# Which products of the MLP stay in PSUM: first and second products of both column groups, in place of four plain sums, with other orders of the pieces

## The chip, the cores and the metric

One core of a Trainium2 chip runs the kernel. The metric is the device time of one execution in microseconds (us); the median of 3 runs before is 1192.7 us.

## The reference

One decoder layer in fp32 over 256 tokens and 16 meta tokens, width D = 2048. After the mixers, which the change does not touch, comes the MLP with 8192 hidden columns:

```python
u = rms_norm(h, g_pre_mlp[l])
f = jnp.square(jax.nn.relu(u @ w_up[l])) @ w_down[l]
h = h + rms_norm(f, g_post_mlp[l])
return h[:, N_META:]
```

## The kernel before

**Numbers.** A weight chunk is 1 MB (128x2048 fp32). SP loads it into one of 5 raw rooms (L1510). ACT rounds it to its high part (`hi`, L1554), DVE subtracts that from the raw chunk (`lo`, L1558). These two halves go into one of four slots: three pairs, and a fourth called `fourth_pair`, which never serves the up projection. TensorE multiplies activations, split in the same way, with both halves.

**The MLP.** Its hidden columns are cut into 8 pieces of 1024. The up projection of a piece has eight chunks U0a0 to U1b1, each 32 matmuls into the banks u0 and u1, which ACT (L1638) and DVE (L1645) read after every second chunk. The down projection has an inner size of 1024 per piece, in two halves, 2 token blocks and 4 column blocks of 512. Of all but the first and the last piece it is done by a seven-product scheme for 2x2 blocks: P1 to P7 for the column blocks 0 and 1, Q1 to Q7 for 2 and 3. Each such product is 12 matmuls 128x512 by `down` (L1771). The weights of P6, P4, Q6 and Q4 are sums that DVE forms in place (L1571, as raw_a<-raw_a,raw_c). Those of P5, P7, Q5 and Q7 are sums that DMAs with an accumulate form, issued on POOL (L1576): the chunk B12, for one, is loaded, then B22 is accumulated onto it, and that is P7's weight. The activations' forms are made by DVE and ACT (L1720 to L1741). X and Y are plain products: 24 matmuls with one raw chunk for both token blocks.

**Banks and sums.** TensorE writes 8 PSUM banks: u0 and u1, four sums x00, x01, x10, x11 for the column blocks 2 and 3 (named acc_up in the trace), and two shared banks a and b. P products go to a and b. After each P product one DVE operation, a *give* (L1804), reads the bank and adds it into `F` in SBUF. Several products add onto what already stands in the bank: P6, P7 and P4 onto a, so that P7 may start only when the give of P6 has read a. Of the Q products Q2, Q3 and Q4 go straight to the x banks. After Q1, Q5, Q6 and Q7 ACT copies bank a or b to SBUF (`st_Q`, L1813), and DVE adds this copy to one or two x banks (L1818). After the last products come squares, a row factor r, and the final multiply-adds with their stores.

**Order.** The strings PLAIN, BLOCKS and LAST_PIECE give the order of products. The class Plan (L23) keeps PE's and SP's order as written and orders the work of DVE, ACT and POOL by costs and by the due times of what waits. An engine works through its list in that order.

Of the kernel before, what the change touches and what calls it, by code (L numbers as in the profile page):

```python
# [15 lines left out]
P = 128  # L16
CK = 4
CW = 512
# [97 lines left out]
def hybrid_block(ctx: ExitStack, tc: tile.TileContext, ins: dict, out: bass.AP):  # L116
# [213 lines left out]
    def load_rows(queue, *names):  # L330
        rows = tmp.tile([48, P], F32, tag="g", name=f"rows_{names[0]}")
# [27 lines left out]
    pre_rows = load_rows(nc.scalar, "g_pre_mix")  # L359
# [13 lines left out]
    other_rows = load_rows(nc.gpsimd, "pool_scale", "b_dw", "conv_ln_g", "conv_ln_b", "g_pre_mlp")  # L373
# [193 lines left out]
    def evac_g(j0):  # L567
        def f(j, acc):
            q = j0 + j
            g = tmp.tile([P, L], F32, tag="g", name=f"g_{q}")  # L570
# [854 lines left out]
    F_raw = big.tile([P, 2 * NT * D // 2], F32, tag="k8", bufs=2, name="F_raw")  # L1425
    F = F_raw[:, :NT * D // 2].rearrange("p (t n c) -> p t n c", t=NT, n=2)

    Q = F_raw[:, NT * D // 2:].rearrange("p (f k t) -> p f k t", f=4, k=KH)
    S3Q, S1Q, S4Q, SQ = range(4)
    S2Q = S3Q  # L1430
    room_of = {}
# [15 lines left out]
    PLAIN = "X3 X1 U0a0+ U0a1+ P1 U0b0+ U0b1+ X2 U1a0+ P5 U1a1+ U1b0+ P3 add:P P6 X4 P7 P2 P4"  # L1447
    BLOCKS = "U0a0+ P1 U0a1+ P5 U0b0+ P6 P3 add:P P7 U0b1+ P4 U1a0+ Q1 P2 Q3 U1a1+ U1b0+ Q5 Q2 add:Q Q6 Q4 Q7"
# [209 lines left out]
    def relu_squared(h, pr, i, s_name, box):  # L1658
# [21 lines left out]
        def q_(f):  # L1680
            return Q[:, f, ks, :]
# [22 lines left out]
    def into_forms(h, pr, i, s_name, box):  # L1704
        G, A, ks = forms[h], f"A{h}{pr}", slice(2 * pr, 2 * pr + 2)

        n = 2 if h or i == NP - 1 or "X1" in MODES[i] else 1

        def dst(part):
            return G[:, A1:A1 + n, ks, part, :]  # L1710

        def src():
            return box["s"].rearrange("p j (f t) -> p f j t", f=2)[:, :n]
        if i < NP - 1 and h == 1:
            def a_(f):
# [19 lines left out]

    def split_form(b, f, name, q, q_name):
        G = forms[b]
        src = [f"{q_name}{pr}" for pr in range(2)]
        plan.add("ACT", 0.53, lambda: nc.scalar.copy(G[:, f, :, 0, :], Q[:, q]),
                 reads=src, writes=(name,))  # L1740
        plan.add("DVE", 0.62, lambda: nc.vector.tensor_sub(  # L1741
            G[:, f, :, 1, :], Q[:, q], f32(G[:, f, :, 0, :])),
            reads=src + [name], writes=(name + "l",))

    def up_done(h, pr, i, accs, acc_names):
        if i == 0:
            n = 2 * h + pr
            up_pair(h, pr, i, accs, acc_names, f"F{n}", lambda: F[:, n // 2, n % 2, :])
# [6 lines left out]
    s_rooms = [Q[:, SQ].rearrange("p k t -> p (k t)")]  # L1755
# [31 lines left out]
    GIVES = {"P1": (0, 0, 1), "P2": (0, 0, 1), "P3": (0, 1, 1), "P4": (1, 0, 1),  # L1787
             "P5": (1, 1, 1), "P6": (0, 1, -1), "P7": (1, 1, -1)}
    GIVES_X = {"Q1": [("x00", 1)], "Q6": [("x10", -1)], "Q7": [("x01", 1), ("x11", -1)],
               "Q5": [("x10", 1), ("x11", 1)]}  # L1790
    given = set()


    def give(s, i):
        t, n, sign = GIVES[s]
        first_ = (t, n) not in given
        given.add((t, n))
        bank, dst, name = banks[BANK[s]], F[:, t, n, :], f"F{2 * t + n}"

        def f():  # L1800
            if first_:
                nc.vector.tensor_scalar_mul(dst, bank, float(sign))
            else:
                (nc.vector.tensor_add if sign > 0 else nc.vector.tensor_sub)(dst, dst, bank)  # L1804
        plan.add("DVE", 0.62, f, reads=(BANK[s], name), writes=(name,))

    def give_x(s):
        box = {}
        bank = BANK[s]

        def save():
            box["st"] = tmp.tile([P, CW], F32, tag="junk", bufs=1, name=f"st_{s}")
            nc.scalar.copy(box["st"], banks[bank])  # L1813
        plan.add("ACT", 0.5, save, reads=(bank,), writes=("junk",))
        for name, sign in GIVES_X[s]:
            def f(dst=banks[name], add_=(nc.vector.tensor_add if sign > 0 else
                                         nc.vector.tensor_sub)):
                add_(dst, dst, box["st"])  # L1818
            plan.add("DVE", 0.62, f, reads=("junk",), writes=(name,))
# [16 lines left out]

    def product_plain(m_, s, i):
        h, n = AT[s]
        for t, f in ((0, A1), (1, A2)):
            name = f"x{n - 2}{t}"  # L1840
            plan.add("PE", 2.72, lambda t=t, f=f, name=name: down(
                banks[name], split_at[m_], h, f, i == 0 and h == 0,
                h == 1 and i == NP - 1 - (n == 3)),
                reads=half_names(m_) + act_names(h, f), writes=(name,))


    LAST_BANK = {(0, 0): "a", (0, 1): "b", (1, 0): "u0", (1, 1): "u1"}

    def product_last(m_, s, i):
        h, n = AT[s]  # L1850
        for t, f in ((0, A1), (1, A2)):
            name = LAST_BANK[n, t]
            plan.add("PE", 2.72, lambda t=t, f=f, name=name: down(
                banks[name], split_at[m_], h, f, h == 0, h == 1),
                reads=half_names(m_) + act_names(h, f), writes=(name,))
        for t in range(NT if h == 1 else 0):
            name, blk = LAST_BANK[n, t], f"F{2 * t + n}"
            plan.add("DVE", 0.62, lambda t=t, name=name: nc.vector.tensor_add(
                F[:, t, n, :], F[:, t, n, :], banks[name]), reads=(name, blk), writes=(blk,))

    def product_block(m_, s, i):
        h, f = FORM[s]
        plan.add("PE", 2.72, lambda: down(banks[BANK[s]], split_at[m_], h, f, s in OPENS, True),
                 reads=half_names(m_) + act_names(h, f), writes=(BANK[s],))
        if s[0] == "P":
            give(s, i)
        elif s in GIVES_X:
            give_x(s)


# [12 lines left out]
    for j in range(4):  # L1883
        plan.add("PE", 1.36, last_of_first(j), reads=(f"hi{q0}", f"lo{q0}"),
                 writes=(f"x{j // 2}{j % 2}",))
# [9 lines left out]
    for pr in range(2):  # L1895
        up_done(0, pr, 0, accs[2 * pr:2 * pr + 2], [f"x{pr}{j}" for j in range(2)])
# [3 lines left out]
    for at_step[0], (s, i) in enumerate(steps):  # L1900
# [18 lines left out]
        {"U": product_up, "X": product_plain, "P": product_block, "Y": product_last,  # L1919
         "Q": product_block}[s[0]](m_, s, i)  # L1920
        m_ += 1
        if (s, i) == ("U1b1", 0):
# [30 lines left out]
    def times_g(t, n):  # L1953
# [3 lines left out]
            reads=(name, f"raw{room_g}"), writes=(f"out{t}{n}", name if n < 2 else f"raw{room_f}"))  # L1957
# [103 lines left out]
```

## Time and profile before

| what | value |
|---|---|
| runs, us | 1189.87, 1192.7, 1196.38 |
| profiled execution | 1189.83 us, of which 1188.1 us span |
| mean granted clock of TensorE | 0.998 |
| PE, DVE, ACT, POOL busy | 1174.9, 1033.6, 688.8, 44.9 us |
| DMA | 272.91 MB, mean 230 GB/s |

The span runs from the first to the last instruction. Busy is the time an engine spends in instructions; of PE the ends are modelled. "a <- b" behind an instruction says which instruction's end released it. The MLP takes about the last 650 us of the span.

### The profile page before, as it was taken

To read this page: it belongs to the slowest core of one execution; us is meant where nothing else is said; L and a number is where in the kernel's file an instruction comes from. 1 tells how busy PE (TensorE), PEld (TensorE's weight loads), DVE (VectorE), ACT (ScalarE), POOL (GpSimd) and SP (SyncE) were. 2 spreads that over 40 slices of the span, in tenths; PEclk is the share of its full clock that TensorE was granted. 3 is DMA by queue.
4 is the path that set the end of the run, shared out by engine and by line. 5 is a ranking of instruction groups with operands and counts; after the bars stand their busy time and mean duration, and the time that the engine had idled before them with its cause. 6 is when DMAs were issued, how large, how long until landed. Compare 5 with 4: busy or idle time off the path is not lost.

```text
span 1188.1 us, 15764 instructions
## 1 busy us (share of the span) xinstructions
PE 1174.9 (99%) x6351; PEld 1018.3 (86%) x6351; DVE 1033.6 (87%) x1106; ACT 688.8 (58%) x712; POOL 44.9 (4%) x51
## 2 busy tenths in 40 slices
PE   9999999999999999999999999999999999999997
PEld 9999988888888878898888888888888888888886
DVE  6899978999776799978988989899999999898965
ACT  6533344444583465665665767666666676666742
POOL 1000000000000001000000000000000000000000
PEclk9999999999999999999999999999999999999999
DMA  9655555655558857858879789898997998998861
GB/s 294 213 179 179 191 196 183 207 178 205 184 156 279 243 210 228 298 167 302 241 209 260 233 250 264 244 274 224 276 254 227 274 271 237 257 259 260 261 250 71
DMA packets 177882, 272.91 MB, mean 230 GB/s; under 512 B 4657, under 2 KB 92913, under 8 KB 176912
## 3 DMA queue, kind: packets, MB, share of 16 engines
q1 hardware_dynamic: 160176, 235.88, 59.4%
q0 software_dynamic: 16736, 34.76, 15.7%
q10 hardware_dynamic: 896, 1.25, 0.3%
q8 instruction: 50, 0.82, 0.3%
q14 instruction: 24, 0.20, 0.0%
HBM read 267.68 MB, written 4.19 MB: 229 GB/s over the span
## 4 chain that ended last, share of the span: by engine, by line
PE 89%; DMA 6%; ACT 2%; DVE 2%; issue 2%; DVEq 0%; POOLq 0%; ACTq 0%
PE bank_u L496 15%; PE acc_gate L800 15%; PE bank_a L1775 9%; PE bank_u L502 7%; PE acc_up L1775 7%; DMA raw_m<-in_w_down_dram 6%; PE bank_b L1775 6%; PE o_c L1168 5%; PE acc_z L491 4%; PE acc_co L800 4%; PE acc_po L800 4%; PE acc_v L491 3%; PE acc_g L491 3%; PE acc_vg L491 2%; PE acc_up L496 1%
## 5 line engine op out<-in xcount | busy, mean ns | idle before, releaser
L496 PE MATMUL bank_u<-m,hi 128*128 128x512 f32 x960 | 329.7, 390 | 0.0
L502 PE MATMUL bank_u<-m,lo 128*128 128x256 f32 x960 | 265.8, 277 | 0.0
L276 ACT CAST hi<-raw 128x2048 fp32r<-128x2048 f32 (+2 forms) x94 | 151.2, 1619 | 189.3 <-PE acc_gate L800 64.0
L1558 DVE TENSOR_TENSOR lo<-raw_m,hi 128x2048 fp32r<-128x2048 f32 x85 | 194.5, 2289 | 35.8 <-ACT hi L1554 35.8
L496 PEld LDWEIGHTS bank_u<-m,hi 128*128 128x128 f32 x960 | 180.4, 188 | 37.9
L279 DVE TENSOR_TENSOR lo<-raw,hi 128x2048 fp32r<-128x2048 f32 (+2 forms) x94 | 180.1, 1925 | 35.4 <-ACT hi L276 35.0
L1554 ACT CAST hi<-raw_m 128x2048 fp32r<-128x2048 f32 x85 | 161.9, 1911 | 69.1 <-PE bank_a L1775 21.9
L502 PEld LDWEIGHTS bank_u<-m,lo 128*128 128x128 f32 x960 | 180.3, 188 | 1.6
L800 PE MATMUL acc_gate<-hi,u_um 128*128 128x512 f32 x416 | 131.2, 390 | 0.0
L557 DVE SCALAR_TENSOR_TENSOR c<-a,taps,c 128x256 f32<-128x256 f32 x240 | 115.6, 483 | 6.8
L800 PEld LDWEIGHTS acc_gate<-hi,u_um 128*128 128x128 f32 x416 | 78.1, 188 | 16.0
L800 PE MATMUL acc_gate<-lo,u_um 128*128 128x512 f32 x208 | 81.1, 390 | 0.0
L1775 PE MATMUL bank_a<-hi,forms 128*128 128x512 f32 (+1 forms) x232 | 75.9, 389 | 2.3 <-DVE F_raw L1804 2.3
L1638 ACT COPY half<-bank_u 128x256 f32<-128x256 f32 x60 | 22.3, 371 | 78.0 <-PE bank_u L502 78.0
L1775 PE MATMUL bank_b<-hi,forms 128*128 128x512 f32 (+1 forms) x208 | 67.5, 386 | 0.0
L1775 PE MATMUL bank_a<-fourth_pair,forms 128*128 128x512 f32 (+1 forms) x252 | 59.9, 387 | 0.7 <-ACT st_Q L1813 0.7
L1558 DVE TENSOR_TENSOR lo<-raw_a,hi 128x2048 fp32r<-128x2048 f32 x21 | 48.0, 2287 | 11.8 <-ACT hi L1554 11.8
L1775 PEld LDWEIGHTS bank_a<-hi,forms 128*128 128x128 f32 x232 | 43.4, 188 | 13.6 <-issue 3.9
L1558 DVE TENSOR_TENSOR lo<-raw_c,hi 128x2048 fp32r<-128x2048 f32 x20 | 45.8, 2288 | 9.4 <-ACT hi L1554 9.4
L1775 PEld LDWEIGHTS bank_a<-fourth_pair,forms 128*128 128x128 f32 x252 | 45.2, 188 | 10.1 <-ACT st_Q L1813 1.1
L1168 PE MATMUL o_c<-hi,m 128*128 128x512 f32 x160 | 50.9, 391 | 0.0
L1554 ACT CAST hi<-raw_a 128x2048 fp32r<-128x2048 f32 x21 | 40.1, 1909 | 18.5 <-PE bank_u L496 10.8
(410 smaller groups left out, 2299.7 us busy)
## 6 DMA issues: line engine op xcount, KB each, us to landing
raw<-in_w_in_dram SPq DMA_DIRECT2D x52, 1024.0 KB, 5.0
raw_m<-in_w_up_dram SPq DMA_DIRECT2D x42, 1024.0 KB, 7.2
raw_m<-in_w_down_dram SPq DMA_DIRECT2D x35, 1024.0 KB, 5.3
raw_a<-in_w_down_dram SPq DMA_DIRECT2D x15, 1024.0 KB, 5.7
raw_c<-in_w_down_dram SPq DMA_DIRECT2D x14, 1024.0 KB, 7.3
raw_m<-in_w_down_dram POOLq DMA_DIRECT2D x12, 1024.0 KB, 11.0
raw_o<-in_w_o_dram SPq DMA_DIRECT2D x10, 1024.0 KB, 5.7
raw_a<-in_w_up_dram SPq DMA_DIRECT2D x9, 1024.0 KB, 7.3
```

What stands on the lines that cost most here:

```text
L276: nc.scalar.copy(hi[:, sl, cs], raw[:, sl, cs])
L279: nc.vector.tensor_sub(lo[:, sl, cs], raw[:, sl, cs], f32(hi[:, sl, cs]))
L491: nc.tensor.matmul(acc, w[:, k[0], cs], act[:, k[1], a, off:], start=first and n == 0, stop=last and n == 2)
L496: nc.tensor.matmul(acc.rearrange("p (a t) -> p a t", a=2)[:, :, ts], hi[:, k[0], cs], act[:, k[1], :, off + ts.start:off + ts.stop], start ...
L502: nc.tensor.matmul(acc[:, :T], lo[:, k[0], cs], act[:, k[1], 0, off:], start=False, stop=stop, skip_group_check=True)
L557: nc.vector.scalar_tensor_tensor(c, conv["a"][:, q, i:i + T], taps[:, q, i:i + 1], c, op0=ALU.mult, op1=ALU.add)
L800: nc.tensor.matmul(acc, act(kk)[:, a_, ts_], w_[:, k, :], start=kk == 0 and n == 0, stop=kk == nk - 1 and n == 2)
L1168: nc.tensor.matmul(acc, form(k, a_), box[w_][:, k, :], start=start and k == 0 and n == 0, stop=stop and k == CK - 1 and n == 2, skip_group ...
L1554: nc.scalar.copy(box["hi"], raw)
L1558: nc.vector.tensor_sub(box["lo"], raw, f32(box["hi"]))
L1638: nc.scalar.copy(box[j], accs[j][:, :T])
L1775: nc.tensor.matmul(acc, forms[h][:, f, k, a_, :], box[w_][:, k, cs], start=start and k == 0 and n == 0, stop=stop and k == KH - 1 and n == ...
```

## The change

The four PSUM sums now hold other things: the running sums of P1 (zp1), P2 (zp2), Q1 (zq1) and Q2 (zq2), over all block pieces. All other block products go to a (6, 7 and 4) and b (5 and 3); 6 and 5 open their bank anew and the others add on. Each is followed by one give from the bank into one of six SBUF sums F(t,n), in both groups alike. The copies st_Q and the adds into PSUM are gone. In the last piece `merge_first` adds zp1 to zp2 and zq1 to zq2 (each an ACT copy and a DVE add) and gives zp1 to three SBUF sums; after the last U1b1 two DVE operations (`merge`) put SBUF sums plus or minus zq1 into u0 and u1, to which the last X products add. The orders PLAIN and BLOCKS are new. A constant tile g2 takes the place of the temporary tile "g", and one form moves to the room "junk". Lines of the changed kernel stand 10 further on in this region.

```diff
-    F_raw = big.tile([P, 2 * NT * D // 2], F32, tag="k8", bufs=2, name="F_raw")
+    F_raw = big.tile([P, 8, CW], F32, tag="k8", bufs=2, name="F_raw")
+    F_AT = {(0, 1): 1, (1, 0): 2, (1, 1): 3, (0, 3): 4, (1, 2): 5, (1, 3): 6}
...
+    Z = ("zp1", "zp2", "zq1", "zq2")
     for j in range(4):
-        banks[f"x{j // 2}{j % 2}"] = accs[j]
+        banks[Z[j]] = accs[j]
...
-    PLAIN = "X3 X1 U0a0+ U0a1+ P1 U0b0+ U0b1+ X2 U1a0+ P5 U1a1+ U1b0+ P3 add:P P6 X4 P7 P2 P4"
-    BLOCKS = "U0a0+ P1 U0a1+ P5 U0b0+ P6 P3 add:P P7 U0b1+ P4 U1a0+ Q1 P2 Q3 U1a1+ U1b0+ Q5 Q2 add:Q Q6 Q4 Q7"
+    PLAIN = "X3 P1 U0a0+ X1 U0a1+ X4 U0b0+ U0b1+ U1a0+ P5 add:P P6 U1a1+ P3 X2 P7 U1b0+ P4 P2"
+    BLOCKS = "P1 U0a0+ U0a1+ Q1 P5 P6 add:P P3 P7 P2 P4 Q5 U0b0+ U0b1+ Q3 Q6 add:Q U1a0+ U1a1+ Q7 U1b0+ Q2 Q4"
...
-    BANK = {"P1": "a", "P6": "a", "P7": "a", "P4": "a", "P5": "b", "P3": "b", "P2": "b"}
-    BANK.update({"Q1": "a", "Q6": "a", "Q7": "a", "Q5": "b", "Q2": "x00", "Q3": "x10",
-                 "Q4": "x01"})
-    OPENS = ("P1", "P5", "P2", "Q1", "Q5")
...
+    BANK_OF = {"6": "a", "7": "a", "4": "a", "5": "b", "3": "b"}
+    COL0 = {"P": 0, "Q": 2}
+    GIVES = {"6": (0, 1, -1), "7": (1, 1, -1), "4": (1, 0, 1), "5": (1, 1, 1), "3": (0, 1, 1)}
...
+    def merge(dst, src, t, n, add_):
+        plan.add("DVE", 0.62, lambda: add_(banks[dst], F(t, n), banks[src]),
+                 reads=(src, f"F{t}{n}"), writes=(dst,))
...
+        start = s[1] in "65" or bank not in begun and bank != "zq2"
...
-        if s[0] == "P":
-            give(s, i)
-        elif s in GIVES_X:
-            give_x(s)
+        if s[1] in GIVES:
+            t, n, sign = GIVES[s[1]]
+            give(bank, t, n + COL0[s[0]], sign)
...
+    def merge_first():
+
+        for g, room, name in (("p", S3Q, "q3"), ("q", S1Q, "q1")):
+            dst, src, held = banks[f"z{g}2"], banks[f"z{g}1"], F_raw[:, room, :]
...
+        if i == NP - 1 and (s[0] != "U" or s == "U1b1") and "merged" not in later:
+            later["merged"] = merge_first()
...
+        if (s, i) == ("U1b1", NP - 1):
+            merge("u0", "zq1", 0, 3, nc.vector.tensor_sub)
+            merge("u1", "zq1", 1, 2, nc.vector.tensor_add)
```

What stands in DVE's list is shown at two places. The first is a middle piece, around the gives of P5, P6 and P7; `lo` rows prepare a product's weights, bank_a and bank_b rows are gives. Before (the rows are lo of P3, lo of P6, give of P5, lo of P7, sum for P4, give of P6, then a lo of the up projection, lo of P4, give of P7):

```order
L1558 TENSOR_TENSOR lo_6769<-raw_m_4557,hi_6762 128x2048
L1558 TENSOR_TENSOR fourth_pair<-raw_a,fourth_pair 128x2048
L1804 TENSOR_TENSOR F_raw<-F_raw,bank_b 128x512
L1558 TENSOR_TENSOR lo_6811<-raw_m_4555,hi_6791 128x2048
L1571 TENSOR_TENSOR raw_a<-raw_a,raw_c 128x2048
L1804 TENSOR_TENSOR F_raw<-F_raw,bank_a 128x512
L1558 TENSOR_TENSOR lo_6843<-raw_m_4556,hi_6825 128x2048
L1558 TENSOR_TENSOR fourth_pair<-raw_a,fourth_pair 128x2048
L1804 TENSOR_TENSOR F_raw<-F_raw,bank_a 128x512
```

After (sum for P4, lo of P3, give of P5, lo of P7, give of P6, lo of P2, lo of P4, give of P7, lo of Q5, give of P3, lo of U0b0, and the two reads of u0 and u1 after U0a1):

```order
L1581 TENSOR_TENSOR raw_m_4546<-raw_m_4546,raw_a 128x2048
L1568 TENSOR_TENSOR lo_6754<-raw_m_4547,hi_6733 128x2048
L1810 TENSOR_TENSOR F_raw<-F_raw,bank_b 128x512
L1568 TENSOR_TENSOR lo_6771<-raw_c,hi_6752 128x2048
L1810 TENSOR_TENSOR F_raw<-F_raw,bank_a 128x512
L1568 TENSOR_TENSOR fourth_pair<-raw_a,fourth_pair 128x2048
L1568 TENSOR_TENSOR lo_6804<-raw_m_4546,hi_6785 128x2048
L1810 TENSOR_TENSOR F_raw<-F_raw,bank_a 128x512
L1568 TENSOR_TENSOR lo_6822<-raw_m_4548,hi_6802 128x2048
L1810 TENSOR_TENSOR F_raw<-F_raw,bank_b 128x512
L1568 TENSOR_TENSOR lo_6838<-raw_m_4547,hi_6819 128x2048
L1655 TENSOR_TENSOR g_99<-half_4_6718,bank_u_4549 128x256
```

The sum for P4, which stood between the lo of P7 and the give of P6, has moved ahead of both; the lo of P2, P4 and Q5 now follow closely on each other.

The second place is the end of the last piece, where the last U1b1 is read out. Before, DVE had there the adds of the last st_Q copies, and then the two reads of u0 and u1:

```order
L1818 TENSOR_TENSOR acc_up_1_4309<-acc_up_1_4309,st_Q_9007 128x512
L1558 TENSOR_TENSOR lo_9039<-raw_m_4556,hi_9009 128x2048
L1725 TENSOR_TENSOR forms_4551<-pairs,forms_4551 128x2x2x128
L1818 TENSOR_TENSOR acc_up_3_4311<-acc_up_3_4311,st_Q_9007 128x512
L1558 TENSOR_TENSOR fourth_pair<-raw_c,fourth_pair 128x2048
L1645 TENSOR_TENSOR pairs<-half_7_9079,bank_u_4558 128x256
L1645 TENSOR_TENSOR pairs<-half_7_9095,bank_u_4559 128x256
```

After, each read (L1655) is followed by a merge that writes the bank just read (L1814; acc_up_2 is zq1):

```order
L1865 TENSOR_TENSOR acc_up_3_4302<-acc_up_3_4302,F_raw 128x512
L1568 TENSOR_TENSOR lo_8944<-raw_a,hi_8940 128x2048
L1810 TENSOR_TENSOR F_raw<-F_raw,bank_a 128x512
L1568 TENSOR_TENSOR lo_8963<-raw_m_4547,hi_8958 128x2048
L1735 TENSOR_TENSOR forms_4542<-pairs,forms_4542 128x2x2x128
L1568 TENSOR_TENSOR fourth_pair<-raw_m_4548,fourth_pair 128x2048
L1655 TENSOR_TENSOR pairs<-half_7_9013,bank_u_4549 128x256
L1814 TENSOR_TENSOR bank_u_4549<-F_raw,acc_up_2_4301 128x512
L1655 TENSOR_TENSOR pairs<-half_7_9030,bank_u_4550 128x256
L1814 TENSOR_TENSOR bank_u_4550<-F_raw,acc_up_2_4301 128x512
```

On ACT the change takes 24 rows away, the st_Q copies, which stood between the hi casts, as here before (copies of the banks of Q5 and Q6):

```order
L1554 CAST hi_7136<-raw_a 128x2048
L1813 COPY st_Q_7140<-bank_b 128x512
L1554 CAST hi_7170<-raw_m_4557 128x2048
L1813 COPY st_Q_7174<-bank_a 128x512
L1554 CAST fourth_pair<-raw_c 128x2048
```

After, nothing stands between the casts of the run of short products:

```order
L1564 CAST fourth_pair<-raw_m_4547 128x2048
L1564 CAST hi_7379<-raw_m_4546 128x2048
L1564 CAST hi_7396<-raw_m_4548 128x2048
L1564 CAST hi_7413<-raw_c 128x2048
L1564 CAST hi_7446<-raw_a 128x2048
```

More of the change, by code (lines that the diff above doesn't have):

```diff
@@ L328, in hybrid_block, with load_rows @@
     vecs = const.tile([P, n_cols], F32, name="vecs")
-    def load_rows(queue, *names):
-        rows = tmp.tile([48, P], F32, tag="g", name=f"rows_{names[0]}")
+    g2 = const.tile([P, 2, L], F32, name="g2")
+    def load_rows(queue, room, *names):
+        rows = g2[:48, room, :P]
         n = 0
@@ L1423, in hybrid_block, with F, q_room @@
         forms.append(room[:, b * LINE:].rearrange("p (f k a t) -> p f k a t", f=4, k=KH, a=2))
[L1425 to L1429 removed]
+    F_raw = big.tile([P, 8, CW], F32, tag="k8", bufs=2, name="F_raw")
+    F_AT = {(0, 1): 1, (1, 0): 2, (1, 1): 3, (0, 3): 4, (1, 2): 5, (1, 3): 6}
+    def F(t, n):
+        return F_raw[:, F_AT[t, n], :]
+    S3Q, S1Q, S4Q = 0, 7, 8
     S2Q = S3Q
+    def q_room(f):
+        if f == S4Q and "s4" not in later:
+            later["s4"] = tmp.tile([P, CW], F32, tag="junk", bufs=1, name="s4_q")
+        return (later["s4"] if f == S4Q else F_raw[:, f, :]).rearrange("p (k t) -> p k t", k=KH)
     room_of = {}
@@ L1737, in split_form @@
         G = forms[b]
-        src = [f"{q_name}{pr}" for pr in range(2)]
-        plan.add("ACT", 0.53, lambda: nc.scalar.copy(G[:, f, :, 0, :], Q[:, q]),
+        src = [f"{q_name}{pr}" for pr in range(2)] + ["junk"] * (q == S4Q)
+        plan.add("ACT", 0.53, lambda: nc.scalar.copy(G[:, f, :, 0, :], q_room(q)),
                  reads=src, writes=(name,))
         plan.add("DVE", 0.62, lambda: nc.vector.tensor_sub(
-            G[:, f, :, 1, :], Q[:, q], f32(G[:, f, :, 0, :])),
+            G[:, f, :, 1, :], q_room(q), f32(G[:, f, :, 0, :])),
             reads=src + [name], writes=(name + "l",))
@@ L1800, in f @@
         def f():
             if first_:
-                nc.vector.tensor_scalar_mul(dst, bank, float(sign))
+                nc.vector.tensor_scalar_mul(dst, src, float(sign))
             else:
[L1804 to L1819, printed above, removed]
+                (nc.vector.tensor_add if sign > 0 else nc.vector.tensor_sub)(dst, dst, src)
@@ L1821, in half_names @@
+        plan.add("DVE", 0.62, f, reads=(bank, name), writes=(name,))
+    def merge(dst, src, t, n, add_):
+        plan.add("DVE", 0.62, lambda: add_(banks[dst], F(t, n), banks[src]),
+                 reads=(src, f"F{t}{n}"), writes=(dst,))
     def half_names(m_):
@@ L1849, in product_last @@
[L1849 to L1859, printed above, removed]
+            if h == 1 and (n, t) not in ((0, 0), (2, 0)) and (i == 0 or n < 2):
+                give(name, t, n)
@@ new lines, in product_block @@
+        if s[1] in GIVES:
[4 more added lines that the diff above has]
+            dst, src, held = banks[f"z{g}2"], banks[f"z{g}1"], F_raw[:, room, :]
+            names = (f"{name}0", f"{name}1")
+            plan.add("ACT", 0.53, lambda held=held, src=src: nc.scalar.copy(held, src),
+                     reads=(f"z{g}1",), writes=names)
+            plan.add("DVE", 0.62, lambda dst=dst, held=held: nc.vector.tensor_add(dst, dst, held),
+                     reads=(f"z{g}2",) + names, writes=(f"z{g}2",))
+        give("zp1", 0, 1, -1)
+        give("zp1", 1, 0)
+        give("zp1", 1, 1, -1)
@@ L1895, in hybrid_block @@
     for pr in range(2):
-        up_done(0, pr, 0, accs[2 * pr:2 * pr + 2], [f"x{pr}{j}" for j in range(2)])
+        up_done(0, pr, 0, accs[2 * pr:2 * pr + 2], Z[2 * pr:2 * pr + 2])
     m_ = 0
```

74 lines of the change are left out of this document (40 added, 34 removed).

## The prediction

> **What bounds the kernel now.** I read the page's busy shares first, then the chain that ended last, PE's waits, and the last 650 us cut into windows around those waits.
>
> ```profile
> PE 1174.9 (99%) x6351; PEld 1018.3 (86%) x6351; DVE 1033.6 (87%) x1106; ACT 688.8 (58%) x712; POOL 44.9 (4%) x51
> PEclk9999999999999999999999999999999999999999
> PE 89%; DMA 6%; ACT 2%; DVE 2%; issue 2%; DVEq 0%; POOLq 0%; ACTq 0%
> ```
>
> TensorE is busy 99% of the span, at the full granted clock in every slice, and makes 89% of the chain. DVE is close behind as a mean. The number of matmuls does not change: the seven-product schemes and the plain products are the same in number and form. So what can go are PE's waits, and what can come are new ones.
>
> ```profile
> PE bank_a L1775 <- DVE F_raw L1804: 2.3, 3, 1.0
> PE idle L392 <- DVE rb L308: 1.1, 1, 1.1
> PE o_a L1168 <- DVE m L925: 0.7, 1, 0.7
> PE bank_a L1775 <- ACT st_Q L1813: 0.7, 1, 0.7
> ```
>
> Of PE's four named waits (us in total, times, longest) two lie before the MLP, which the change leaves as it is. Two are waits for the bank a: three times for a give, once for an st_Q copy. These are exactly the things that the change rearranges.
>
> ```profile
> 748.50:750.00 1.50, 1.46 (x7) 0.91 (x6) 1.50 (x3) 1.24 (x1) 0.00 (x0) 1.00 1.01 393
> 750.00:830.50 80.50, 80.50 (x420) 68.90 (x419) 73.50 (x62) 53.89 (x52) 5.09 (x4) 1.00 0.90 253
> 830.50:833.00 2.50, 1.75 (x8) 1.20 (x7) 2.50 (x3) 1.36 (x1) 0.00 (x0) 1.00 0.95 297
> 913.50:916.00 2.50, 1.48 (x8) 0.93 (x7) 2.50 (x3) 1.20 (x1) 0.00 (x0) 1.00 0.94 274
> 996.50:999.00 2.50, 1.99 (x9) 1.35 (x9) 2.50 (x3) 1.52 (x1) 0.00 (x0) 1.00 0.93 312
> 1128.50:1131.00 2.50, 1.83 (x9) 1.19 (x8) 2.50 (x2) 2.15 (x4) 0.00 (x0) 1.00 1.04 336
> 1131.00:1179.72 48.72, 48.72 (x246) 41.44 (x244) 30.96 (x42) 18.38 (x28) 0.00 (x0) 1.00 0.43 154
> 1179.72:1188.10 8.38, 0.00 (x0) 0.00 (x0) 3.81 (x10) 0.77 (x3) 0.00 (x0) 0.69 0.43 155
> ```
>
> Columns: stretch, length, busy PE, PEld, DVE, ACT, POOL, clock, DMA share, GB/s. PE lacks 0.04, 0.75, 1.02, 0.51 and 0.67 us in five short stretches, 2.99 us together; between them it is busy without a gap. While it waits DVE is busy all the time. The last 8.4 us hold no matmul: the row factor and the stores, after the last product.
>
> **What one stall is made of.** The chain that ends in the stall near 998 us:
>
> ```profile
> 968.18 10.48 DMA raw_m<-in_w_down_dram
> ...
> 979.28 11.60 DMA raw_m<-in_w_down_dram
> ...
> 990.95 1.92 ACT hi L1554
> ...
> 992.93 2.02 issue
> ...
> 995.10 2.28 DVE raw_a L1571
> 997.39 0.61 DVE F_raw L1804
> ...
> 998.13 2.08 PE bank_a L1775 x8
> ```
>
> The chunk B12 is loaded (10.48 us), B22 is accumulated onto it (11.60), ACT rounds it (1.92), DVE forms the lo of P7 (the 2.02 shown as issue), then the sum for P4 (2.28), then the give of P6 (0.61), for which P7 waits. P7's own weights are there 2.9 us before; it waits because DVE put the sum ahead of the give.
>
> ```profile
> 831.16 0.39 PE L1775 MATMUL bank_b<-hi,forms 128*128 128x512 f32 x1
> 832.30 0.47 PE L1775 MATMUL bank_a<-hi,forms 128*128 128x512 f32 x1 [0.75 <-DVE F_raw L1804]
> 832.60 0.39 PE L1775 MATMUL bank_a<-lo,forms 128*128 128x512 f32 x1
> 832.83 0.62 PE L1775 MATMUL bank_a<-hi,forms 128*128 128x512 f32 x2
> ```
>
> From start to start a matmul takes 0.23 us (832.60 to 832.83). Across the stall it is 1.14, which is 0.91 lost, and 0.30 behind it, another 0.07: 0.98 in all where the window lacks 0.75. So each stall costs 0.23 more than its idle time, and the five cost 2.99 + 5 x 0.23 = 4.1 us.
>
> **The change part by part.**
>
> ```profile
> L1818 DVE TENSOR_TENSOR acc_up<-acc_up,st_Q 128x512 f32<-128x512 f32 x36 | 24.4, 693 | 0.0
> L1804 DVE TENSOR_TENSOR F_raw<-F_raw,bank_a 128x512 f32<-128x512 f32 x26 | 17.7, 682 | 0.0
> L1804 DVE TENSOR_TENSOR F_raw<-F_raw,bank_b 128x512 f32<-128x512 f32 x19 | 12.9, 681 | 0.0
> L1813 ACT COPY st_Q<-bank_a 128x512 f32<-128x512 f32 x18 | 10.4, 580 | 3.5 <-DVE acc_up L1818 3.2 <-PE bank_a L1775 0.3
> L1813 ACT COPY st_Q<-bank_b 128x512 f32<-128x512 f32 x6 | 3.5, 575 | 0.0
> L1558 DVE TENSOR_TENSOR lo<-raw_m,hi 128x2048 fp32r<-128x2048 f32 x85 | 194.5, 2289 | 35.8 <-ACT hi L1554 35.8
> L1645 DVE TENSOR_TENSOR pairs<-half,bank_u 128x256 f32<-128x256 f32 x42 | 17.5, 416 | 2.8 <-ACT half L1638 2.6
> ```
>
> *Gives and copies.* A middle piece has 7 gives and 6 adds before, 10 gives after: three operations at 0.69 us fewer, 2.1 us of DVE per piece. On ACT the 24 copies go, 13.9 us. Neither engine is the bound as a mean, so nothing of this counts by itself. It counts through the places where PE waits.
>
> *The give of P6.* P7 still follows P6 in bank a with one product, P3, between, 12 x 0.23 = 2.7 us. The sum for P4 now stands ahead of the lo of P7. So the chain loses its 2.28 us at this place, and gains nothing. B12's load is issued when a room comes free, by my count of the new order 28.6 us before P7's start; with the durations of the chain above P7 is ready after 10.5 (load) + 0.5 (to the issue on POOL) + 11.6 (accumulate) + 1.9 (hi) + 2.2 (lo) + 0.7 (give of P6) + 0.1 (to PE) = 27.5. That leaves 1.1 us. The stalls at 832, 915 and 998 go: 0.98 + 1.25 + 0.74 = 3.0 us. The small one at 749 is of the same kind (0.3).
>
> *The st_Q stall.* At 1130 PE waits for a copy behind hi casts on ACT (0.9 with the restart). No copy is left there, and Q4 and Q7 in bank a now stand two or three products apart. It goes.
>
> ```profile
> 977.79 2.29 DVE L1558 TENSOR_TENSOR lo<-raw_c,hi 128x2048 fp32r<-128x2048 f32 x1
> 979.99 2.29 DVE L1558 TENSOR_TENSOR lo<-raw_a,hi 128x2048 fp32r<-128x2048 f32 x1
> ```
>
> *The eight short products.* Two lo of DVE behind one another stand 2.2 us apart, as do sums. Q1 P5 P6 P3 P7 P2 P4 Q5 now come without an up chunk between. They last 8 x 2.72 = 21.8 us and each wants its own lo, besides the sums for P6 and P4, four gives, a few form operations: 25 to 27 us of DVE. Up to three products stand prepared in other slots when the run begins, some 6.6 us of lo. So DVE falls behind by 3 to 5 us of a cover of 6.6, and catches up under the up chunks (5.4 us of PE for one lo of 2.2). Walked through row by row with the durations above, counted from the start of Q1: the give of P5 is done at 6.4, wanted at 8.2; of P6 at 9.2, wanted at 10.9; of P7 at 14.3, wanted at 16.3; of P3 at 17.1, wanted at 19.1; the reads of u0 and u1 at 20.0, wanted at 21.8. The slack is 1.7 to 2.0 us everywhere. My value is no stall. Bounds: 0, and at most one lo (2.29) in each of six pieces, 13.7 us.
>
> *The accumulates.* The number (4 per piece) stays. Now B12's and X1's are issued one behind the other, where before the pair shared the queue less often.
>
> ```profile
> raw_m<-in_w_down_dram POOLq DMA_DIRECT2D x12, 1024.0 KB, 11.0
> raw_m<-in_w_down_dram POOLq DMA_DIRECT2D x1, 1024.0 KB, 15.2
> raw_m<-in_w_down_dram SPq DMA_DIRECT2D x35, 1024.0 KB, 5.3
> ```
>
> The median accumulate lands after 11.0 us (first row, the page). In a window near 640 us, where two were issued 3 us apart, the second took 15.2. Plain loads have a median of 5.3, half of what the chain above had. With medians B12 lands at about 0 in the walk and may land at 4.9; X1's accumulate lands some 9 later and may land at 14.2. With the chain's slow load both are just in time. I take no stall; bounds 0 and some 2.5 per piece.
>
> *PLAIN.* The first block piece and the plain one have the same kinds of work in another order; the smallest slack I find is about 1 us, before U1a0. None; bounds 0 and 2.
>
> *The last piece.* Two ACT copies, two DVE adds, three gives of zp1 (0.69 each) fall beside up chunks and plain products. The merges stand between the reads of u0 and u1 and X1's second half, which adds onto u1: after U1b1 0.37 + 0.42 + 0.42 on ACT and DVE and 2 x 0.69, all under the 2.72 us of X1's first half, with 1.1 us to spare if no lo cuts in. None; bounds 0 and 2.3. The tail after the last matmul keeps its form: 8.4 us.
>
> *Sum.* 1189.83 - 3.0 - 0.3 - 0.9 = 1185.7 us, against the profiled execution's own time. That is a ratio of 0.9965. Against the median of 1192.7 it is 1188.6 us. The three runs lie up to 0.3% off their median; 0.5%, 6 us, is about what a measurement of this kernel can tell from no change. PE's waits in the MLP sum to 4.1 us, so this change can hardly reach that bound by its own means.
>
> **A rule that speaks against the change.** The chain and the wait rows above show PE waiting on one shared bank until DVE has read it. The Trainium skill, Perfetto Trace Analysis, section Matmuls, wants independent matmul groups to rotate through different PSUM banks so that the read-out of one overlaps the next group. Of this kernel's stalls all five fit that rule. The change leaves two rotating banks and gives all ten read-outs of a piece to them. By the rule the stalls should stay or grow, to the sum of rival A below (1201.8). By the walk above the distance between two users of a bank (one other product, 2.7 us) is enough.
>
> **The rivals.**
>
> *A. Slower: the run of eight falls behind.* If DVE or the accumulates are later than walked by more than 1.7 us, every bank of the run waits in turn: the give of P6 behind the lo of P7, P7 behind it, P2 and P4 behind theirs, and the queue has no up chunk in which to recover before Q5. The price is what exceeds the slack, up to one lo of 2.29, in each of six pieces. For it: DVE's list is in order, DVE is 91% busy (73.50 of 80.50) in a middle piece, and the slow load of the chain would use up the whole margin. Against it: three operations and all ACT copies fewer per piece. With 2.2 us in each of six pieces it is 6 x 2.2 = 13.2 more, 1188.6 + 13.2 = 1201.8. It decides from 0.7 us per piece (4.1 / 6), beyond which the gain is eaten.
>
> *B. Nothing: the wait goes to the next in line.* The accumulate, not the sum for P4, is the longest part of the chain. If B12 or X1 lands 1 to 2 us later than before, P7 or Q5 waits for its weights in place of its bank, some 0.7 us in each of six pieces: 1188.6 + 4.1 = 1192.7.
>
> *C. The change does not do what it says.* The products in zp1 to zq2 no longer need a read-out, but 6, 7 and 4 still share bank a. The stalls at P7 stay if DVE's order on the chip puts something else ahead of the give. The order of the lists is fixed, so this is the least likely: about 1192.
>
> **How the numbers follow.** Forecast (no stall, or little): 0.50, 1186 to 1190. B and C together: 0.25, 1190 to 1195. A: 0.25, 1195 to 1203. For the range I reach from 1184 into A up to 1202. Of the forecast's half about a quarter falls beyond 0.5% by the scatter of the runs and a tail that is a little shorter: 0.13 faster. B, C and the rest of the forecast: 0.63 the same. A from 1198.7 on: 0.24 slower.
>
> **What would show it.** Right: PE's wait rows for bank_a gone or under 0.3 us, PE busy in all windows of the middle pieces, DVE at about 89% there (2.1 of 81 us fewer), no st_Q on ACT, a tail of 8.4. Wrong: rows of PE waiting for DVE F_raw (the give, now at L1810), for a lo (L1568), or for a DMA into raw_m; a wait that returns six times with a period of 82 us points to A or B, and the engine that it names tells which.

## The result, and the profile after

| | before | after |
|---|---|---|
| median, us (6 runs each) | 1192.78 (1189.87 to 1196.38) | 1185.1 (1184.52 to 1186.39) |
| ratio, 95% interval | | 0.994 [0.9921, 0.9959] |
| profiled execution, its span | 1189.83, 1188.1 | 1184.91, 1183.2 |

The changed kernel is 0.6% faster, 7.7 us by medians and 4.9 us by the two profiled executions. The runs also lie closer together: 1.9 us from the shortest to the longest, against 6.5 before.

The page of the kernel after, first the busy times, then the chain that ended last:

```profile
PE 1172.7 (99%) x6351; PEld 1018.9 (86%) x6351; DVE 1027.6 (87%) x1095; ACT 679.3 (57%) x690; POOL 45.1 (4%) x51
...
PE 99%; DVE 0%; ACT 0%; issue 0%; DVEq 0%; ACTq 0%
```

The number of matmuls is the same. The chain, of which PE made 89% before, with loads, casts and sums of weights in the rest, is now almost PE alone. All of PE's named waits (us in total, times, longest):

```profile
PE idle L394 <- DVE rb L308: 1.1, 1, 1.1
PE o_a L1170 <- DVE m L927: 0.7, 1, 0.7
```

Both lie ahead of the MLP and were there before. The two rows of waits for bank_a are gone. The windows of the MLP (stretch, length, busy PE, PEld, DVE, ACT, POOL, clock, DMA share, GB/s):

```profile
533.00:741.00 208.00, 208.00 (x1094) 178.75 (x1093) 184.99 (x172) 132.91 (x138) 11.43 (x9) 1.00 0.88 253
741.00:822.80 81.80, 81.80 (x425) 70.06 (x425) 74.28 (x61) 53.27 (x49) 5.11 (x4) 1.00 0.91 257
822.80:837.00 14.20, 14.20 (x64) 11.74 (x64) 14.20 (x11) 8.26 (x5) 0.00 (x0) 1.00 0.86 291
837.00:1120.00 283.00, 283.00 (x1479) 243.16 (x1478) 258.03 (x209) 185.13 (x169) 16.50 (x13) 1.00 0.91 260
```

PE is busy without a gap. The third row is a part of the run of eight short products in one piece: DVE is busy for all of its 14.20 us, and still in time. DVE's list there, and the first PE rows of P7 and P4 behind it:

```profile
823.27 0.68 DVE L1810 TENSOR_TENSOR F_raw<-F_raw,bank_b 128x512 f32<-128x512 f32 x1
823.87 2.28 DVE L1568 TENSOR_TENSOR lo<-raw_c,hi 128x2048 fp32r<-128x2048 f32 x1
826.07 0.68 DVE L1810 TENSOR_TENSOR F_raw<-F_raw,bank_a 128x512 f32<-128x512 f32 x1
826.67 2.28 DVE L1568 TENSOR_TENSOR fourth_pair<-raw_a,fourth_pair 128x2048 fp32r<-128x2048 f32 x1
828.87 2.28 DVE L1568 TENSOR_TENSOR lo<-raw_m,hi 128x2048 fp32r<-128x2048 f32 x1
831.08 0.68 DVE L1810 TENSOR_TENSOR F_raw<-F_raw,bank_a 128x512 f32<-128x512 f32 x1
```
```profile
827.85 0.39 PE L1785 MATMUL bank_a<-hi,forms 128*128 128x512 f32 x1
...
833.29 0.39 PE L1785 MATMUL bank_a<-hi,forms 128*128 128x512 f32 x1
```

The give of P6 ends at 826.75, and P7 starts in bank a at 827.85: 1.10 us later, of which a wait that is only just met takes 0.15 (the give that P7 waited for in the stalls of before ended 0.15 ahead of it). The give of P7 ends at 831.76, and P4, which waits for it, starts 1.5 us later. The same distances come again in the next piece. They hang on DVE's list, in which no row here has a wait, and not on a landing.

### The profile page after: what moved, and what is told of

Its sections match the earlier page's. It is cut to its first block, busy times and chain, and to the rows that moved or that the text cites. A ratio compares the mean times of both kernels' runs of the same rounds, so it can differ in the third digit from the quotient of the medians.

```text
span 1183.2 us, 15774 instructions
## 1 busy us (share of the span) xinstructions
PE 1172.7 (99%) x6351; PEld 1018.9 (86%) x6351; DVE 1027.6 (87%) x1095; ACT 679.3 (57%) x690; POOL 45.1 (4%) x51
## 3 DMA queue, kind: packets, MB, share of 16 engines
q10 hardware_dynamic: 896, 1.25, 0.3%
## 4 chain that ended last, share of the span: by engine, by line
PE 99%; DVE 0%; ACT 0%; issue 0%; DVEq 0%; ACTq 0%
PE bank_u L498 18%; PE acc_gate L802 15%; PE bank_a L1785 10%; PE bank_u L504 9%; PE acc_up L1785 8%; PE bank_b L1785 7%; PE o_c L1170 5%; PE acc_z L493 4%; PE acc_co L802 4%; PE acc_po L802 4%; PE acc_v L493 3%; PE acc_g L493 3%; PE acc_vg L493 2%; PE acc_up L498 1%; PE bank_u L1785 1%; PE o_a L1170 1%
## 5 line engine op out<-in xcount | busy, mean ns | idle before, releaser
L1568 DVE TENSOR_TENSOR lo<-raw_m,hi 128x2048 fp32r<-128x2048 f32 x70 | 160.1, 2287 | 31.5 <-ACT hi L1564 31.4
L1564 ACT CAST hi<-raw_m 128x2048 fp32r<-128x2048 f32 x70 | 133.8, 1912 | 73.7 <-DVE raw_m L1581 21.3
L1785 PE MATMUL bank_a<-hi,forms 128*128 128x512 f32 (+1 forms) x288 | 93.5, 386 | 0.0
L1568 DVE TENSOR_TENSOR lo<-raw_a,hi 128x2048 fp32r<-128x2048 f32 x29 | 66.3, 2286 | 10.8 <-ACT hi L1564 10.7
L1564 ACT CAST hi<-raw_a 128x2048 fp32r<-128x2048 f32 x29 | 55.4, 1910 | 35.3 <-PE bank_u L498 13.8
L1564 ACT CAST hi<-raw_c 128x2048 fp32r<-128x2048 f32 x27 | 51.5, 1907 | 27.1 <-PE bank_u L498 11.8
L1568 DVE TENSOR_TENSOR lo<-raw_c,hi 128x2048 fp32r<-128x2048 f32 x27 | 61.7, 2285 | 5.2 <-ACT hi L1564 5.1
L1568 DVE TENSOR_TENSOR fourth_pair<-raw_m,fourth_pair 128x2048 fp32r<-128x2048 f32 x26 | 59.4, 2286 | 4.4 <-ACT fourth_pair L1564 4.4
L1785 PE MATMUL acc_up<-hi,forms 128*128 128x512 f32 x176 | 57.5, 390 | 0.0
L1785 PE MATMUL bank_a<-lo,forms 128*128 128x512 f32 (+1 forms) x144 | 55.6, 386 | 0.0
```

What stands on the lines that cost most here:

```text
L1564: nc.scalar.copy(box["hi"], raw)
L1568: nc.vector.tensor_sub(box["lo"], raw, f32(box["hi"]))
L1785: nc.tensor.matmul(acc, forms[h][:, f, k, a_, :], box[w_][:, k, cs], start=start and k == 0 and n == 0, stop=stop and k == KH - 1 and n == ...
```

## The experiments

Two theories were put against each other. O: the order of DVE's list made the stalls (the sum for P4 ahead of the give of P6). B: the freed banks did it, by fewer read-outs and no copies.

**before_again, before_third: the kernel before, two more profiles.**

> The kernel before, unchanged, with a second profile. The forecast of a gain of 4.1 us came from the profile of an execution that was the shortest of six (1189.83 us; the median is 1192.78), and the gain by medians is 7.7 us. Theory V: PE's stalls in the MLP vary from run to run with the landing of the accumulates, and the runs above 1190 us have more of them. Then PE's lost time in the MLP (4.2 us of stalls in the first profile) is larger here by about as much as the time is above 1190: a run of 1193 us shows some 7 us of waits for bank_a and for weights. Rival: the stalls are fixed at 4.2 us and the rest of the difference lies ahead of the MLP or in the tail; then PE's wait rows for bank_a sum to 3.0 us again, whatever the time.

> A third profile of the kernel before. The second had 1188.6 us and lost 3.3 us to four stalls where the first, at 1189.8, lost 4.2 to five, not at the same pieces. Theory V (the stalls behind the accumulates vary): the lost time is again different, and time minus stalls is the same 1185.3 to 1185.6 us as in those two. Rival: another part of the execution varies, and time minus stalls moves by over 0.7 us.

They took 1188.6 and 1190.02 us. PE's waits for bank_a in the first, then in the second:

```profile
PE bank_a L1775 <- DVE F_raw L1804: 1.6, 3, 0.7
...
PE bank_a L1775 <- ACT st_Q L1813: 0.7, 1, 0.7
```
```profile
PE bank_a L1775 <- DVE F_raw L1804: 1.9, 3, 0.7
...
PE xt L432 <- DMA x_in<-in_x_dram: 0.8, 1, 0.8
PE bank_a L1775 <- ACT st_Q L1813: 0.7, 1, 0.7
```

The give stalls vary in size and place: three in each of the two, near 749, 996 and 1079 us, where the first profile had them at 749, 832, 915 and 998. The st_Q wait is the same each time. With restarts PE loses 4.2, 3.3 and 3.6 us.

The landing of the accumulate for P7's weights decides which pieces stall. Take the last five block pieces in each of the three profiles. In ten of these fifteen the accumulate took 11.1 to 12.9 us from issue to landing; P7 then always starts some 7.26 us after the landing, with a stall. In the other five it took 9.6 to 10.9 us, and P7 waits for nothing.

Time minus the stalls is 1185.6, 1185.3 and 1186.4. So the rest varies too, by 1.1 us, which is more than the 0.7 that the rival named. Of this, 0.8 is the wait of the third for its first load (the xt row), far ahead of the MLP, that the others lack. The first half of theory V, that the stalls vary with the accumulates, holds. Its second half does not follow: no profiled execution was above 1190.02, while the median of the kernel is 1190.9 to 1192.8 in every group of runs, and that the longer ones have more of the same stalls was not seen in a trace.

**banks_old_order: the new banks, old orders.**

```diff
-    BLOCKS = "P1 U0a0+ U0a1+ Q1 P5 P6 add:P P3 P7 P2 P4 Q5 U0b0+ U0b1+ Q3 Q6 add:Q U1a0+ U1a1+ Q7 U1b0+ Q2 Q4"
+    BLOCKS = "U0a0+ P1 U0a1+ P5 U0b0+ P6 P3 add:P P7 U0b1+ P4 U1a0+ Q1 P2 Q5 U1a1+ U1b0+ Q3 Q2 add:Q Q6 Q7 Q4"
```

> The changed kernel's banks and read-outs (three DVE operations per piece fewer, no copies on ACT) with the orders of before, but for two exchanges that the shared banks need (Q5 ahead of Q3, Q7 ahead of Q4). DVE then has the sum for P4 again between the lo of P7 and the give of P6. Theory O (the order of DVE's list makes the stall): P7's stalls stay, 0.7 to 1.3 us in most block pieces, and only the st_Q stall goes: 1188 to 1191 us, PE waiting for bank_a <- DVE F_raw some 2 to 5 us. Theory B (fewer read-outs free DVE, 2.1 us per piece): the give comes 2 us earlier and the stalls go: 1185 us.

Measured: 1236.78 us, ratio 1.0387 [1.0369, 1.0405]. Neither theory: the edit itself made new waits. PE at Q6 and Q7, then PE's waits:

```profile
802.37 0.39 PE L1785 MATMUL bank_a<-hi,forms 128*128 128x512 f32 x1
803.63 0.47 PE L1785 MATMUL bank_a<-hi,forms 128*128 128x512 f32 x1 [0.87 <-DVE F_raw L1810]
```
```profile
PE bank_a L1785 <- DVE F_raw L1810: 14.0, 12, 2.4
PE bank_b L1785 <- DVE fourth_pair L1568: 11.5, 6, 2.2
PE bank_b L1785 <- ACT fourth_pair L1564: 6.7, 5, 2.4
```

Q6, Q7 and Q4 follow each other in bank a here. Ten of these twelve successions cost 1.0 to 1.3 us each (802.37 to 803.63 is 1.26 where a matmul here takes 0.23 from start to start), the other two 2.0 and 2.5. And Q5, whose weights are made by an accumulate onto Q1's chunk, follows Q1 with only P2 between; PE waits for both halves of them (the fourth_pair rows). How much of that is the accumulate and how much the lists of ACT and DVE was not taken apart.

**p7_apart: the banks of before, P6 and P7 moved apart.**

```diff
-    BLOCKS = "U0a0+ P1 U0a1+ P5 U0b0+ P6 P3 add:P P7 U0b1+ P4 U1a0+ Q1 P2 Q3 U1a1+ U1b0+ Q5 Q2 add:Q Q6 Q4 Q7"
+    BLOCKS = "U0a0+ P1 U0a1+ P5 U0b0+ P6 P3 add:P U0b1+ P7 U1a0+ P4 P2 Q1 Q3 U1a1+ U1b0+ Q5 Q2 add:Q Q6 Q4 Q7"
```

> The kernel before with its banks, copies and read-outs; only BLOCKS is changed: U0b1 is put between P3 and P7, U1a0 between P7 and P4, so that P6 and P7 in bank a are 8 us apart in place of 2.7. Theory O: P7's stalls go, and the time falls by what they were, to 1185 to 1189 us, with the st_Q stall perhaps left (0.9). Theory B: the work of DVE and ACT is as before, so nothing goes, or the wait moves to another product: 1191 to 1194 us.

Measured: 1225.14 us, ratio 1.0291 [1.0276, 1.0307]. The give waits are gone from PE's list, as O says, but a larger one came:

```profile
PE bank_u L496 <- DVE pairs L1645: 25.4, 4, 6.8
```

DVE at one of the four, and a link of its chain:

```profile
860.95 0.42 DVE L1725 TENSOR_TENSOR forms<-pairs,forms 128x256 fp32r<-128x256 f32 x1
868.00 2.29 DVE L1558 TENSOR_TENSOR fourth_pair<-raw_m,fourth_pair 128x2048 fp32r<-128x2048 f32 x1 [6.64 <-ACT fourth_pair L1554]
870.21 0.41 DVE L1645 TENSOR_TENSOR pairs<-half,bank_u 128x256 f32<-128x256 f32 x1
```
```profile
849.36 16.64 DMA raw_m<-in_w_down_dram
```

Q1 comes one product closer to Q5, the accumulate between them lands 16.6 us after its issue, DVE waits 6.6 us for Q5's weights, and the read of u0 stands behind that lo in its list. The mechanism of the forecast's rival B, a product that waits for weights because their accumulate lands late, is seen here at Q5; the change kept clear of it.

**banks_old_order2 and banks_old_order3: the same with a mended Q part.** The lines show the end of BLOCKS, in this order: banks_old_order, banks_old_order2, banks_old_order3.

```diff
-U1a0+ Q1 P2 Q5 U1a1+ U1b0+ Q3 Q2 add:Q Q6 Q7 Q4
+U1a0+ Q1 P2 Q5 U1a1+ U1b0+ Q6 Q3 add:Q Q7 Q2 Q4
+U1a0+ Q1 P2 U1a1+ U1b0+ Q5 Q6 add:Q Q3 Q7 Q2 Q4
```

> The changed kernel's banks with the order of before in the P part of each piece, and a Q part that keeps one product between two users of bank a (Q1 P2 Q5 U1a1 U1b0 Q6 Q3 Q7 Q2 Q4), which banks_old_order did not: there Q6, Q7 and Q4 followed each other in bank a, and PE waited 1.03 and 1.29 us for a give each time. If those direct successions made its waits for F_raw, 14 us of them, they go to under 3 us here. Theory O: P7's irregular waits stay (DVE's list has the sum between again); theory B (three read-outs fewer): no wait for F_raw at P7. Waits for fourth_pair, 18 us there, come from how the slots rotate in this Q part, and may stay: 1186 to 1210.

> The changed kernel's banks and read-outs with the order of before up to U1b0, in which Q5 comes where it came before (behind U1b0), so that the accumulate for its weights has time, and bank a is never used twice in a row: U0a0 P1 U0a1 P5 U0b0 P6 P3 P7 U0b1 P4 U1a0 Q1 P2 U1a1 U1b0 Q5 Q6 Q3 Q7 Q2 Q4. DVE has the sum for P4 between the lo of P7 and the give of P6 again. Theory O (DVE's order at P7 makes the stall, the banks do not remove it): P7 waits for DVE F_raw as in the three profiles of before, 0.6 to 1.2 us in about half of the pieces; 1187 to 1191 us, if the new Q part adds no wait of its own. Theory B (fewer read-outs are enough): no wait for F_raw at P7, 1185 us.

banks_old_order2 took 1220.5 us, ratio 1.0251 [1.0233, 1.027]. With one product between two users of bank a the 14.0 us fall to 0.4:

```profile
PE bank_b L1785 <- DVE fourth_pair L1568: 11.9, 6, 2.2
PE bank_b L1785 <- ACT fourth_pair L1564: 5.4, 5, 1.1
...
PE bank_a L1785 <- DVE F_raw L1810: 0.4, 1, 0.4
```

banks_old_order3 took 1191.46 us, ratio 1.000 [0.9986, 1.0013]: the new banks with nearly the old order bring nothing. But the loss is not where O put it. Its waits on PE in the MLP:

```profile
PE bank_b L1785 <- DVE lo L1568: 0.5, 1, 0.5
PE bank_u L498 <- DVE pairs L1655: 0.3, 2, 0.2
```

By starts of matmuls PE loses 4.7 us in the MLP, about as much as in the profiles of before. Of this 1.0 is at P7, in four pieces (0.14 to 0.19 each, with DVE's give just met, and 0.08 behind it), 1.4 at P5, whose weights come from an accumulate, and 2.1 at u0 and u1. So fewer read-outs and no copies are not enough. Whether they help P7 is not shown: in these four pieces the accumulate for its weights also lands 8.0 to 11.4 us ahead of it, where the stalls of before had 7.26. Since the order of the Q part is also not that of before, this test is not clean.

**sum_first: one row of DVE's list moved, in the kernel before.**

```diff
+            u = uses.pop(n4)
+            uses.insert(n7, (uses[n7][0],) + u[1:])
...
+        plan.add("DVE", 2.22, low, reads=names + [f"hi{q}"] + first, writes=(f"lo{q}",))
```

> The kernel before with its banks, copies and orders; only the sum for P4 is moved ahead: DVE does it in front of the lo of P7, which now waits for it, so that nothing but that lo stands ahead of the give of P6. Theory O (the sum between lo and give makes P7 wait): P7's waits for DVE F_raw, 1.6 to 2.3 us and their restarts in the profiles of before, are gone in all middle pieces; the st_Q wait (0.95 with restart) is left; 1186 to 1188 us, and the runs lie closer together. Theory L (the accumulate lands late, and whatever stands behind it is late too): P7 then waits for its lo in place of the give, and the time stays at 1190 to 1192.

Measured: 1187.41 us (1187.06 to 1188.55, 10 runs), ratio 0.9972 [0.9962, 0.9981]. The only wait for a bank that is left:

```profile
PE bank_a L1783 <- ACT st_Q L1821: 0.7, 1, 0.7
```

With all 13 read-outs and the copies in place, the give stalls are gone but for 0.2 us near 750, and the runs lie within 1.5 us. That is theory O. The edit moves a little more than one row: the chunk that the sum needs is also loaded one place earlier, and other chunks change rooms. So one could think that the accumulate for P7 lands earlier. It does not. The cast of P7's weights on ACT and P7's first matmul, at the same place in the kernel before and in sum_first:

```profile
825.11 1.91 ACT L1554 CAST hi<-raw_m 128x2048 fp32r<-128x2048 f32 x1 [2.00 <-DMA raw_m<-in_w_down_dram]
832.30 0.47 PE L1775 MATMUL bank_a<-hi,forms 128*128 128x512 f32 x1 [0.75 <-DVE F_raw L1804]
```
```profile
827.04 1.91 ACT L1561 CAST hi<-raw_a 128x2048 fp32r<-128x2048 f32 x1 [3.21 <-DMA raw_a<-in_w_down_dram]
832.11 0.40 PE L1783 MATMUL bank_a<-hi,forms 128*128 128x512 f32 x1
```

In both the cast waits for the landing. Before, P7 starts 7.19 us after the cast, with a stall; in sum_first 5.07 us after it, with none. In three pieces of sum_first the accumulate took 12.7 to 13.2 us, longer than all but one of those that made a stall before, and P7 lost 0.2 us at most. The sum's 2.2 us are what the chain from the landing to P7 has lost.

**sum_first_y and after_again: the st_Q wait, and the distance that is left.**

```diff
-    LAST_BANK = {(0, 0): "a", (0, 1): "b", (1, 0): "u0", (1, 1): "u1"}
+    LAST_BANK = {(0, 0): "b", (0, 1): "a", (1, 0): "u0", (1, 1): "u1"}
```

> sum_first with one more exchange: Y1's first half goes to bank b and its second to a (before: a, then b). In the profiles of before and of sum_first the st_Q wait stands where Y1 opens bank a right behind Q7, with no product between; ACT copies Q7's bank only after its last matmul. Theory O': this direct succession makes that wait, not the casts ahead on ACT; it goes, 0.95 us less than sum_first, 1186.4 us, and the copies and adds that are left cost nothing. Theory B' (the copies on ACT and the 13 read-outs as such cost time): the wait moves or stays, 1187.4, and the changed kernel stays over 2 us ahead.

> The changed kernel, unchanged, on the same chip as sum_first_y, so that the two can be told apart to under half a microsecond. Theory O': 1185.1 to 1185.6 us, about 1 us under sum_first_y, of which up to 1 us is the many waits under 0.06 us that the profiles sum to 0.9 to 1.5 us here and 2.1 in sum_first. Theory B': over 2 us under it.

Measured, on one chip: 1186.07 us, ratio 0.9952 [0.994, 0.9965], and 1185.16 us, ratio 0.9941 [0.9929, 0.9953], where before had 1192.83. PE's waits in sum_first_y are the two ahead of the MLP and no other. So the wait at 1130 us was the direct succession of Q7 and Y1 in bank a, and two small exchanges in the old kernel give 6.8 of the 7.7 us. Between the first and the last matmul of the MLP the profiles have 642.15 us in sum_first_y and 641.00 in after_again; no wait over 0.06 us is in either. Of these 1.1 us, 0.6 lie in the first 128 matmuls of the MLP. They take 21.8 us in after and after_again and 22.4 in sum_first_y, but also 22.4 in late_give1, which is the changed kernel up to there, and 21.8 in before_again, which is the old one. So these 0.6 us differ between executions, not between the kernels. Where the rest lies was not settled.

**late_give3 and late_give1: how much room the changed kernel has.**

```diff
+                for _ in range(extra):
+                    nc.vector.tensor_scalar_mul(dst, dst, 1.0)
...
+            give(bank, t, n + COL0[s[0]], sign, 3 if s == "P6" else 0)
```

> The changed kernel with three more DVE operations (F times 1.0, 0.6 us each from start to start) ahead of the give of P6 in every piece: 1.8 us. In the profile after, P7 starts 1.10 us after the give of P6 is done, in every middle piece. Theory: this slack is real and belongs to DVE's list; then PE waits 0.7 us for the give of P6 in each of six pieces, and 0.08 behind: 4.7 us, 1190 us. Rival: the slack is larger, because DVE's list has idle time elsewhere that takes the delay up, or smaller, because what follows (lo of P2 and P4, the give of P7, slack 1.5) is pushed too: 1185 in the one case, 1192 or more in the other.

> The changed kernel with one DVE operation of 0.6 us ahead of the give of P6, where late_give3 has three. With three, PE lost 0.50 + 0.08 us in each of six pieces, so the slack would be 1.8 - 0.5 = 1.3, near the 1.10 that the profile after shows with 0.15 us of semaphore time. By that one operation costs nothing: 1185 us. If the loss is not a threshold but grows with the work of DVE, a third of late_give3's 3.9 us: 1186.4.

Measured: 1189.01 us, ratio 0.9982 [0.9972, 0.9993], with three; 1185.61, ratio 0.9958 [0.9945, 0.9971], with one. DVE in late_give3, and PE's wait:

```profile
827.52 1.34 DVE L1811 TENSOR_SCALAR F_raw<-F_raw 128x512 f32<-128x512 f32 x3
828.97 0.69 DVE L1812 TENSOR_TENSOR F_raw<-F_raw,bank_a 128x512 f32<-128x512 f32 x1
```
```profile
PE bank_a L1785 <- DVE F_raw L1812: 2.0, 6, 0.3
```

The three operations delay the give by 1.45 us (827.52 to 828.97), not by 1.8 as expected. By starts of matmuls PE loses 0.50 at P7 and 0.08 behind it, in six pieces: 3.5 us, and 3.9 by medians. 1.45 - 0.50 = 0.95 is the room, which is the 1.10 of the trace less 0.15. One operation fits in, and PE's wait list is that of the kernel after.

## Why the prediction was right, and where its size was off

*No stall left, none new: right.* The profiled execution was forecast at 1185.7 us and came out at 1184.91. All five stalls are gone, and sum_first shows the step named for the give of P6, the sum for P4 out of its way, to be enough by itself. That the time came out 0.8 us shorter is partly luck: the first 128 matmuls of the MLP took 22.4 us in the profile before and 21.8 in the one after, a difference that comes and goes between executions.

*The st_Q stall: it went, for another reason.* The forecast put it down to the casts ahead on ACT. It stood where Y1 opened the bank that Q7 had just filled; sum_first_y took it away and left all casts and copies. In the changed kernel Y1 starts in zp2, so this succession is gone.

*The run of eight: right, with less room.* Forecast slacks were 1.7 to 2.0 us, the trace has 1.1 to 1.5, and late_give3 confirms 0.95 to the first loss. DVE's share of a middle piece stayed at 91%, not 89%. It does three operations fewer per piece, as forecast, and is busy for 74.13 us where it was 75.90; but the piece itself became shorter too, 81.65 us in place of 83.16.

*The accumulates: earlier than the bounds.* In a window around the issue of the accumulates of B12 (raw_c) and X1 (raw_m), and P7's cast on ACT:

```profile
raw_c<-in_w_down_dram POOLq DMA_DIRECT2D x1, 1024.0 KB, 8.6
raw_m<-in_w_down_dram POOLq DMA_DIRECT2D x1, 1024.0 KB, 12.9
```
```profile
819.89 1.91 ACT L1564 CAST hi<-raw_c 128x2048 fp32r<-128x2048 f32 x1 [0.68 <-PE acc_up L1785]
```

B12 was issued at 808.02, so it lands at 816.6, 3.3 us ahead of the cast, which waits for PE to free the slot. X1's is issued at 808.77 and lands at 821.7, 6.4 us ahead of its cast (828.05, for Q5).

*PLAIN, the last piece, the tail: right.* PE waits for nothing in them, and the merges cost nothing that shows. From the end of the last matmul the tail takes 8.65 us, where 8.4 was forecast.

*The rule on banks: it did not decide here.* Ten read-outs go through two banks and PE does not wait. The Trainium skill's rule in Perfetto Trace Analysis, section Matmuls, that groups should rotate through banks, is seen in the two extremes: no product between two users of a bank costs 1.0 us or more each time (banks_old_order), one product of 2.7 us between is enough if DVE's list has the give in time.

*The step that failed in size: the carry-over to the median.* The prediction took 4.1 us from one profile, made a ratio of 0.9965 of it, and put that on the median. The measured ratio is 0.994, beyond the bound of 0.5%, to which the forecast had given 0.13. The profiled execution, at 1189.83 us, was as short as the shortest of the six runs, and its stalls were taken as the kernel's. The later profiles show them to vary, and the kernels whose give stalls are gone, or the same in every piece, run within 0.8 to 1.9 us (late_give1, late_give3, sum_first, after; one run of sum_first_y was 2.3 above the rest), while the kernel before spreads over 4.3 to 6.8 in every group. The gain by medians holds the stalls of the median run, some 2 to 3 us more. This last part is argued from the spread; no trace of a long run was had.

## What to carry to other kernels

A product that reuses a bank waits for its read-out, and the read-out stands in an engine's list. Look for what stands ahead of it there, and move that, before giving out banks anew; two small exchanges gave most of the gain here. Leave one other product between two users of a bank, and as much time between a chunk's first use and its accumulated reuse as a slow accumulate takes. When the waits that are to go hang on DMA landings, the spread of the runs says more of the gain than one profile does, and a profile of a short run can understate it.

## What the runs showed of the hardware that was not expected

TensorE ran at half its rate after a stretch of some 4 us with almost no matmul. In banks_old_order, around two waits for weights with one matmul between:

```profile
775.00:779.20 4.20, 0.98 (x4) 0.24 (x2) 4.20 (x2) 3.91 (x4) 0.00 (x0) 1.00 0.85 301
779.20:780.40 1.20, 1.12 (x5) 0.94 (x6) 1.17 (x2) 0.00 (x0) 0.64 (x1) 1.00 0.92 259
780.40:783.80 3.40, 3.40 (x10) 2.61 (x9) 3.40 (x3) 0.37 (x1) 0.63 (x1) 0.51 0.97 229
783.80:790.00 6.20, 6.20 (x39) 5.48 (x38) 4.26 (x6) 2.74 (x4) 0.00 (x0) 1.00 1.09 265
```

PE is busy for 0.98 of 4.2 us; then come 1.2 us at the full granted clock, 3.4 us at 0.51, and again the full clock. By this (3.4 us at about half the rate) the waits cost some 1.7 us more than their own length, an estimate. The Trainium skill, TensorE: Matmul & The Clock Gate, Part 1, tells of a gate that halves the clock when the array has been idle and needs about 3.4 us of work to open; the 3.4 us here agree. The stalls of before, 1.25 us at most, left the clock at 1.00.

On DVE F times 1.0, from SBUF to SBUF, takes 0.42 us for 128x512 (late_give1), where the give takes 0.68. It is not the PSUM bank alone that makes the give slower. In the kernel after, an operation with one input from a bank and one with two inputs from SBUF take as long as the give (mean ns behind the comma):

```profile
L1808 DVE TENSOR_SCALAR F_raw<-bank_a 128x512 f32<-128x512 f32 x3 | 2.0, 683 | 0.0
L1751 DVE TENSOR_TENSOR forms<-F_raw,forms 128x512 fp32r<-128x512 f32 x21 | 13.9, 684 | 0.0
```
